# Shifting where a matmul kernel's buffers stand in SBUF, by multiples of 64 bytes

## The chip, the cores and the metric

The kernel runs on one core of a Trainium2 chip. The metric is the device time of one execution in microseconds; 1243.23 us is the median of two runs of the kernel before (1243.19 to 1243.27). One more execution was taken with the hardware profiler and is the source of every row below.

## The reference

Two transformer-like blocks run one after the other on 256 tokens of width 1024, in float32. Cut to what matters:

```
# first block
h = rmsnorm(x); proj = h @ w_in                       # 1024 x 8192
branches = conv mixer, stick-breaking attention, retention   # each 512 wide
x = x + (sum_n sigmoid(gates_n) * (branch_n @ w_branch_n)) @ w_o
x = x + memory_attention(rmsnorm(x), rmsnorm(mem), w_xq, w_xkv, w_xo)
x = x + relu(rmsnorm(x) @ w_up)**2 @ w_down           # 1024 x 4096 x 1024
x = rmsnorm(x)
# second block
h = layer_norm(a*h + ssd_mixer(h))                    # in 1024 x 6176, out 2048 x 1024
h = layer_norm(a*h + conv_ffn(h))                     # up 1024 x 5632, down 2816 x 1024
h = layer_norm(a*h + mla_attention(h))                # latents 384 and 256 wide
h = layer_norm(a*h + conv_ffn(h))
```

## The kernel before, in words

**Three matmuls for one.** Each float32 operand is held as a high part in the float32r format and a rest. A product is formed as high x high, high x rest and rest x high, accumulated in PSUM (`mm3`, with `passes = ((0, 0), (0, 1), (1, 0))`). Every one of these matmuls loads its own stationary operand of 128 columns (LDWEIGHTS) and then streams 256 or 512 moving columns of 4 bytes.

**The weights.** They come from DRAM in about 200 chunks of up to 128 x 2048 elements, through three rings that `pump`, `copy` and `sub` serve: `wr` (raw, two buffers, by DMA), `wh` (high parts, four buffers, written by ScalarE) and `wl` (rests, four buffers, written by VectorE). Method `ring` makes each buffer; each is 8192 bytes of a partition.

**Which operand streams.** In `wstat` the weights are loaded and the activations stream, 256 columns at a time: this is the up projections, gates, queries and keys. In `xstat` the activations are loaded and the weights stream, mostly 512 columns at a time: this is the down and output projections. `wmixed` does the first three chunks of an up projection with streaming weights of 256 columns.

**The activations.** `new_act` gives each layer a pair `ah`, `al` (128 x 8 x 256 elements each, high and rest). It is called seven times: for the mixers, the memory attention's queries, the MLP, the SSD mixer, the first FFN, the latent attention, the second FFN. Other stationary or moving operands have pairs of their own: `br` (the three branches), `mt` (merged) and `memT` (the memory), `gT` (the hidden layer of MLP and FFN), `yT` (SSD), `oT` (attention outputs), `cT` (latents).

**The order of the work.** A planner in the program (`Plan`, `tick`, `step`) decides, when the program is built, in which order each engine's instructions are written; it uses modelled costs and never a buffer's address. The buffers' addresses follow from the order in which the pools are opened and from `gap`, which allocates so many unused bytes.

**A word used below.** The *place* of a buffer is its byte address in a partition, modulo 512. Before, `wr`, `wh` and `wl` all stand at place 288, `ah` and `al` at 480, `br`, `gT`, `yT` and the memory attention's `oT` at 288, `mt`, `memT`, `cT` and the latent attention's `oT` at 480. The *distance* of an operand is its place minus that of `wh`, modulo 512. Within a buffer, a step from one 128-row slice to the next is a multiple of 512 bytes in every case named here, so one distance holds for a whole stage.

Of the kernel before, what the change touches and what calls it, by code (L numbers as in the profile page):

```python
# [7 lines left out]
F32R = mybir.dt.float32r  # L8
# [8 lines left out]
P = 128  # L17
D = 1024
S = 256
ALPHA = 4 ** 0.25  # L20
NG = 8
RAW, HELD = 2, 4
# [198 lines left out]
class Slots:  # L221
    def __init__(self, kern, pool, name, shape, dtype, n):
        self.kern, self.at, self.pool, self.name, self.shape, self.dtype = kern, kern.at, pool, name, shape, dtype
        self.idle = list(range(n))
        self.out, self.old, self.lent = {}, {}, {}
# [237 lines left out]
        self.sync = Lane(plan, nc.sync, "sp")  # L463


class Kern:
    def __init__(self, nc, tc, a, dbg=None):
        self.at = Plan()
        self.nc, self.tc, self.a, self.dbg = Engines(nc, self.at), tc, a, dbg
        self.plan, _ = chunk_plan()  # L470
        self.nch = len(self.plan)
        self.n_dma = self.n_prep = self.n_half = self.n_get = self.n_done = 0
        self.raw, self.held, self.subs = {}, {}, []
        self.bg = []
        self.floor = 0.0
        self.turns = {}
        self.blocked, self.table = False, None
        self.work = self.skew = 0.0
        self.sums = np.concatenate([[0.0], np.cumsum([len(ks) * max(n, P) * UNIT for _, ks, _, n, _ in self.plan])])

# [12 lines left out]
            self.n_dma += 1  # L493

    def ring(self, pool, tag, dtype, n):
        t = pool.tile([P, 2048], dtype, tag=tag, name=tag)
        rows = self.turns.setdefault(tag, [])
        self.at.reuse(t, rows[-n] if len(rows) >= n else None)
        rows.append(t)
        return t  # L500
# [316 lines left out]

    def new_act(self):

        return (self.acts.tile([P, 8, S], F32R, tag="ah", name="ah"), self.acts.tile([P, 8, S], F32R, tag="al", name="al"), [0, 0])  # L820

    def ready(self, act, k, *taus):
        if len(act) == 3:
# [132 lines left out]
    def mixers(self, act):  # L956
        nc, a = self.nc, self.a
        mp, mp_close = self.open("mix")
        br = self.pair(mp, "br", 12)
        gt = Slots(self, mp, "gt", [P, 3, S], F32, 4)  # L960
        r256 = Slots(self, mp, "r256", [P, 256], F32, 6)
# [267 lines left out]
        for m in range(8):  # L1229
            wh, wl = self.get("br")  # L1230
# [534 lines left out]
    def attention(self, h, act):  # L1765
        nc = self.nc
        cos, sin = self.cs[:, 0], self.cs[:, 1]
        pool, close = self.open("mla")
        self.gap(pool, 704)
        cT = self.pair(pool, "cT", 5)  # L1770
        krT = pool.tile([P, S], F32, tag="krT", name="krT")
        knT = pool.tile([P, 8, S], F32, tag="knT", name="knT")
# [100 lines left out]
        for tau in range(2):  # L1873
            for tag, nk, src, blocks in (("qr", 3, cq, [(0, 512)]), ("v", 2, ckv, [(0, 512), (512, D)])):
                if tau == 0:
                    chs[tag] = self.get(tag)
                wh, wl = chs[tag]
# [90 lines left out]
    def program(self):  # L1968
        nc, tc, a = self.nc, self.tc, self.a
        cs = []  # L1970

        def pool(name, bufs=1, **kw):
            cm = tc.tile_pool(name=name, bufs=bufs, **kw)
            cs.append(cm)
            return cm.__enter__()

        cp = pool("const")
        self.gb = pool("gb", 2)  # L1980
        self.dram = pool("dram", space=bass.MemoryType.DRAM)
        self.acts = pool("acts")
        cq = pool("small")
        self.tiny = pool("tiny", 4)
        self.tk = Slots(self, pool("tk"), "tk", [P, D], F32, 2)
        self.wraw, self.whi, self.wlo = pool("wraw", RAW), pool("whi", HELD), pool("wlo", HELD)
        pp = pool("ps", space=PSUM)
        self.mm = Slots(self, pp, "mm", [P, 512], F32, 4)
        self.sm = Slots(self, pp, "sm", [P, 512], F32, 4)

        x = cp.tile([P, 2, D], F32, tag="x", name="x")
        self.cst = cst = cq.tile([P, NCST], F32, tag="cst", name="cst")
        self.ones = cp.tile([P, P], F32, tag="ones", name="ones")
        nc.vector.memset(self.ones, 1.0)

        row = self.tk.get()
        o, w = ROWS["mix"]
        nc.sync.dma_start(out=row[0:1, :], in_=a["prow"][0:1, o:o + w])
        halves = [slice(512 * n, 512 * n + 512) for n in range(2)]
        for c in halves:  # L2000
            nc.sync.dma_start(out=x[:, 0, c], in_=a["x"][0:P, c])
        nc.sync.dma_start(out=cst[:, 0:P], in_=a["cst"][:, 0:P])
        self.pump(1)
        nc.sync.dma_start(out=x[:, 1, :], in_=a["x"][P:2 * P, :])
        self.pump()
        nc.sync.dma_start(out=cst[:, P:], in_=a["cst"][:, P:])
        gs = [self.mm.get() for c in halves]
        for pt, c in zip(gs, halves):
            self.mm1(pt, self.ones[0:1, :], row[0:1, c], True)
        self.tk.put(row)  # L2010
        self.pcol = cp.tile([P, NCOL], F32, tag="pcol", name="pcol")
        nc.sync.dma_start(out=self.pcol, in_=a["pcol"])
        self.ident, self.nu, self.ut = (cst[:, CST[n]:CST[n] + P] for n in ("ident", "nu", "ut"))
        self.at.one = cq.tile([1, 2], F32, tag="one", name="one")
        nc.vector.memset(self.at.one, 1.0)
        self.neg1 = cp.tile([P, P], F32, tag="neg1", name="neg1")
        nc.vector.memset(self.neg1, -1.0)
        self.mhalf = cq.tile([P, 2], F32, tag="mhalf", name="mhalf")
        nc.vector.memset(self.mhalf, -0.5)
        self.identb = cp.tile([P, P], BF16, tag="identb", name="identb")  # L2020
        nc.vector.tensor_copy(self.identb, self.ident)

        self.maskb = cp.tile([P, P], BF16, tag="maskb", name="maskb")
        nc.vector.memset(self.maskb, 0.0)
        nc.gpsimd.affine_select(out=self.maskb, in_=self.maskb, compare_op=ALU.is_ge, fill=-1e30, base=0,
                                pattern=[[-1, P]], channel_multiplier=1)

        act = self.new_act()
        self.until(self.spawn(self.rms(0, x, Halves(gs), act), first=True))

        def second():
            yield from self.rms(1, x, Halves(gs), act)
            for pt in gs:
                self.mm.put(pt)

        self.spawn(second(), first=True)
        mt, memT, mt_close = self.mixers(act)
        self.spawn(self.angles(cp))
        act, close = self.memory(x, mt, memT, mt_close)
        act = self.mlp(x, act, close)  # L2040
        act = self.ssd(x, act)
        act = self.ffn(0, x, act)
        act = self.attention(x, act)
        self.ffn(1, x, act)
        self.drain()
        assert self.n_get == self.nch
        for cm in reversed(cs):
            cm.__exit__(None, None, None)
# [21 lines left out]
```

## Time and profile before

| | |
|---|---|
| median of two runs | 1243.23 us |
| the profiled execution | 1244.83 us, span 1243.1 us |
| TensorE (PE) | 1224.7 us busy, 8468 matmuls |
| weight loads (PEld) | 1120.8 us busy, beside the matmuls |
| VectorE (DVE) | 853.9 us busy |
| ScalarE (ACT) | 717.0 us busy |
| DMA | 227.71 MB, mean 183 GB/s |

A matmul's row shows its start and its modelled duration, 0.28 us for 256 columns; it overlaps the next one's. The pace of a stretch is therefore the time from one start to the next, not the duration. Where a row gives a stretch and a count, the count also holds the two matmuls or so that were under way at the stretch's start.

### The profile page before, as it was taken

The page shows a single profiled execution, that of the slowest core. Times are in us where ns is not written, and L with a number is a line of the kernel's source. Part 1 is how long each engine was busy: PE and PEld are TensorE (multiplying, and loading weights), DVE is VectorE, ACT ScalarE, POOL GpSimd, SP SyncE. Part 2 cuts the span into 40 slices and gives each one's busy share as a digit, 9 for nine tenths or more (in the row PEclk, how much of TensorE's full clock was granted, in tenths as well). Part 3 has the DMA queues.
Part 4 walks back from the last instruction along what each step waited for, and adds up shares of the span by engine and source line. Part 5 has one row for each costly group of instructions (what it writes and reads, how often), then busy time and mean ns, then how long its engine had stood idle before and what let it go on. Part 6 is the DMA issues. An engine that isn't in the chain of part 4 may idle for free.

```text
span 1243.1 us, 20768 instructions
## 1 busy us (share of the span) xinstructions
PE 1224.7 (99%) x8468; PEld 1120.8 (90%) x8468; DVE 853.9 (69%) x1378; ACT 717.0 (58%) x1181; POOL 53.5 (4%) x85
## 2 busy tenths in 40 slices
PE   7999999999999999999999999999999999999997
PEld 5978999989989998889999898999988888999986
DVE  5666847666746665446787797877765866888853
ACT  5666546446536554335788765666644575666641
POOL 0011000000000000000111201000000000000000
PEclk9999999999999999999999999999999999999999
DMA  7643355546544546524656555555573443455560
GB/s 254 235 167 127 146 196 219 179 156 228 176 152 159 214 172 221 201 106 166 227 190 233 193 174 194 187 172 202 184 259 118 161 181 123 172 197 182 213 256 35
DMA packets 35425, 227.71 MB, mean 183 GB/s; under 512 B 4321, under 2 KB 4993, under 8 KB 11522
## 3 DMA queue, kind: packets, MB, share of 16 engines
q1 hardware_dynamic: 35330, 226.39, 50.8%
q8 instruction: 66, 1.08, 0.4%
q14 instruction: 29, 0.24, 0.1%
HBM read 225.27 MB, written 1.10 MB: 182 GB/s over the span
## 4 chain that ended last, share of the span: by engine, by line
PE 95%; DVE 3%; DMA 1%; issue 0%; ACT 0%; POOL 0%; SPq 0%; POOLq 0%; DVEq 0%; ACTq 0%
PE mm L284 85%; PE sm L284 9%; DVE wl L284 1%; DVE x L284 1%; DMA wr<-wts 0%; DVE tk L284 0%; DMA cst<-cst 0%; POOL rs L284 0%; ACT wh L284 0%; DVE ln L284 0%; DVE al L284 0%; SPq L284 0%; POOLq L2066 0%; ACT r L284 0%; ACT ah L284 0%
## 5 line engine op out<-in xcount | busy, mean ns | idle before, releaser
L284 DVE TENSOR_TENSOR wl<-wr,wh 128x1024 fp32r<-128x1024 f32 (+3 forms) x408 | 479.4, 1198 | 173.7 <-ACT wh L284 173.0
L284 ACT CAST wh<-wr 128x1024 fp32r<-128x1024 f32 (+3 forms) x408 | 403.6, 1029 | 162.4 <-PE mm L284 87.9
L284 PE MATMUL mm<-ah,wh 128*128 128x256 f32 (+1 forms) x1496 | 421.1, 281 | 0.0
L284 PE MATMUL mm<-ah,wl 128*128 128x256 f32 (+1 forms) x1496 | 417.5, 279 | 0.0
L284 PE MATMUL mm<-al,wh 128*128 128x256 f32 (+1 forms) x1496 | 417.4, 279 | 0.0
L284 PEld LDWEIGHTS mm<-ah,wh 128*128 128x128 f32 (+1 forms) x1496 | 283.0, 189 | 1.6 <-issue 1.1
L284 PEld LDWEIGHTS mm<-ah,wl 128*128 128x128 f32 (+1 forms) x1496 | 281.0, 188 | 0.1
L284 PEld LDWEIGHTS mm<-al,wh 128*128 128x128 f32 (+1 forms) x1496 | 280.5, 188 | 0.4
L284 DVE SCALAR_TENSOR_TENSOR r<-mm,pcol,r 128x255 f32<-128x255 f32 (+2 forms) x212 | 86.9, 474 | 38.6 <-ACT r L284 38.6
L284 PE MATMUL mm<-wl,ah 128*128 128x512 f32 (+3 forms) x320 | 106.3, 338 | 3.1 <-DVE wl L284 3.0
L284 PE MATMUL mm<-wh,ah 128*128 128x512 f32 (+3 forms) x320 | 108.6, 345 | 0.0
L284 PE MATMUL mm<-wh,al 128*128 128x512 f32 (+3 forms) x320 | 105.9, 337 | 0.5 <-DVE al L284 0.5
L284 PE MATMUL mm<-wh,gTh 128*128 128x512 f32 x304 | 96.3, 391 | 0.0
L284 PE MATMUL mm<-wh,gTl 128*128 128x512 f32 x304 | 95.6, 389 | 0.0
L284 PE MATMUL mm<-wl,gTh 128*128 128x512 f32 x304 | 95.6, 390 | 0.0
L284 ACT ACTIVATE r<-mm,pcol 128x256 f32<-128x256 f32 x96 | 48.9, 560 | 46.9 <-PE mm L284 46.9
L284 PEld LDWEIGHTS mm<-wl,ah 128*128 128x128 f32 x320 | 60.3, 189 | 10.2 <-DVE wl L284 4.9
L284 PEld LDWEIGHTS mm<-wh,gTl 128*128 128x128 f32 x304 | 57.1, 188 | 11.8
L284 PEld LDWEIGHTS mm<-wl,gTh 128*128 128x128 f32 x304 | 57.1, 188 | 11.8
L284 PEld LDWEIGHTS mm<-wh,gTh 128*128 128x128 f32 x304 | 56.7, 188 | 12.0 <-issue 0.6
L284 PEld LDWEIGHTS mm<-wh,al 128*128 128x128 f32 x320 | 60.3, 189 | 7.0 <-DVE al L284 1.1
L284 PEld LDWEIGHTS mm<-wh,ah 128*128 128x128 f32 x320 | 60.3, 189 | 6.6 <-issue 0.7
(296 smaller groups left out, 1581.8 us busy)
## 6 DMA issues: line engine op xcount, KB each, us to landing
wr<-wts SPq DMA_DIRECT2D x186, 1024.0 KB, 4.9
wr<-wts SPq DMA_DIRECT2D x11, 768.0 KB, 4.3
gb<-prow SPq DMA_DIRECT2D x12, 512.0 KB, 6.8
dec<-rows SPq DMA_DIRECT2D x8, 768.0 KB, 7.5
wr<-wts SPq DMA_DIRECT2D x4, 704.0 KB, 4.2
wr<-wts SPq DMA_DIRECT2D x4, 512.0 KB, 7.0
tk<-mem SPq DMA_DIRECT2D x2, 512.0 KB, 7.9
out<-x SPq DMA_DIRECT2D x4, 256.0 KB, 2.1
```

The lines of the kernel that those rows point to most:

```text
L284: r = f(*args, **kw)
```

## The change: what it does

No instruction is added, removed or moved: the program that is built holds the same instructions in the same order with the same waits on every engine. Only addresses change.

- `ring` makes each `wl` buffer 64 bytes longer (`PLACE` elements of 4 bytes), so the four stand at places 480, 32, 96 and 160. With `gap0` in front, `wr` and `wh` stand at 480; all four of each still do.
- `new_act` allocates 128 elements more and lets the layer's activations begin `PLACES[n]` bytes further on, with another value for each of its seven calls. The high part and the rest move alike.
- Gaps of 320 bytes place the branches `br` and the latents `cT` (with the latent attention's `oT`) at 288.
- The scratch for dynamic DMA descriptors is cut from 16384 to 1024 bytes, which makes the room.

Distances from `wh` (bytes, modulo 512), worked out from the allocations of the two programs:

| operand | before | after |
|---|---|---|
| `ah`, `al`: mixers, memory queries | 192 | 64, 64 |
| `ah`, `al`: MLP | 192 | 320 |
| `ah`, `al`: SSD | 192 | 192 |
| `ah`, `al`: first FFN | 192 | 448 |
| `ah`, `al`: latent attention | 192 | 0 |
| `ah`, `al`: second FFN | 192 | 128 |
| `br` | 0 | 320 |
| `cT`, latent attention's `oT` | 192 | 320 |
| `mt`, `memT` | 192 | 0 |
| `gT`, `yT`, memory attention's `oT` | 0 | 0 |
| `wl`, by ring position | 0, 0, 0, 0 | 0, 64, 128, 192 |

```
+PLACE = 16
+PLACES = (64, 64, 320, 192, 448, 0, 128)
...
+        self.n_act = 0
...
     def ring(self, pool, tag, dtype, n):
-        t = pool.tile([P, 2048], dtype, tag=tag, name=tag)
+        t = pool.tile([P, 2048 + (PLACE if tag == "wl" else 0)], dtype, tag=tag, name=tag)
...
     def new_act(self):
-        return (self.acts.tile([P, 8, S], F32R, tag="ah", name="ah"), self.acts.tile([P, 8, S], F32R, tag="al", name="al"), [0, 0])
+        at = PLACES[self.n_act] // 4
+        self.n_act += 1
+        h, l = (self.acts.tile([P, 8 * S + 128], F32R, tag=n, name=n)[:, at:at + 8 * S].rearrange("p (k s) -> p k s", s=S) for n in ("ah", "al"))
+        return (h, l, [0, 0])
...
         mp, mp_close = self.open("mix")
+        self.gap(mp, 320)
         br = self.pair(mp, "br", 12)
...
         pool, close = self.open("mla")
-        self.gap(pool, 704)
+        self.gap(pool, 320)
...
-        self.wraw, self.whi, self.wlo = pool("wraw", RAW), pool("whi", HELD), pool("wlo", HELD)
+        self.gap(pool("gap0"), 192)
+        self.wraw, self.whi = pool("wraw", RAW), pool("whi", HELD)
+        self.wlo = pool("wlo", HELD)
+        self.gap(pool("gap1"), 256)
...
-    nc = bacc.Bacc("TRN2", target_bir_lowering=False, num_devices=1)
+    nc = bacc.Bacc("TRN2", target_bir_lowering=False, num_devices=1, dynamic_dma_scratch_size=1024)
```

## Rows read from the trace of the kernel before

**Rows 1.** The page's head and the engines' busy time (share of the span).
```profile
span 1243.1 us, 20768 instructions
...
PE 1224.7 (99%) x8468; PEld 1120.8 (90%) x8468; DVE 853.9 (69%) x1378; ACT 717.0 (58%) x1181; POOL 53.5 (4%) x85
```

**Rows 2.** The page's chain that ended last: shares of the span by engine, by line.
```profile
PE 95%; DVE 3%; DMA 1%; issue 0%; ACT 0%; POOL 0%; SPq 0%; POOLq 0%; DVEq 0%; ACTq 0%
PE mm L284 85%; PE sm L284 9%; DVE wl L284 1%; DVE x L284 1%; DMA wr<-wts 0%; DVE tk L284 0%; DMA cst<-cst 0%; POOL rs L284 0%; ACT wh L284 0%; DVE ln L284 0%; DVE al L284 0%; SPq L284 0%; POOLq L2066 0%; ACT r L284 0%; ACT ah L284 0%
```

**Rows 3.** Matmul groups by form, one of three passes each (shape, xcount | busy us, ns).
```profile
L284 PE MATMUL mm<-ah,wh 128*128 128x256 f32 x1488 | 418.9, 281 | 0.0
...
L284 PE MATMUL mm<-wh,gTh 128*128 128x512 f32 x304 | 96.3, 391 | 0.0
...
L284 PE MATMUL mm<-wh,ah 128*128 128x512 f32 x144 | 59.0, 410 | 0.0
...
L284 PE MATMUL mm<-wh,ah 128*128 128x256 f32 x144 | 41.0, 285 | 0.0
...
L284 PE MATMUL mm<-brh,wh 128*128 128x256 f32 x96 | 27.3, 285 | 0.0
...
L284 PE MATMUL mm<-memTh,wh 128*128 128x256 f32 x64 | 17.8, 278 | 0.0
```

**Rows 4.** Stretches of one kind: us, busy PE (matmuls), granted clock, DMA share, GB/s.
```profile
140.00:180.00 40.00, 40.00 (x355) 1.00 0.56 198
198.00:208.00 10.00, 10.00 (x87) 1.00 0.68 264
238.00:250.00 12.00, 12.00 (x102) 1.00 0.58 199
282.00:295.00 13.00, 13.00 (x117) 1.00 0.48 181
384.00:390.00 6.00, 6.00 (x54) 1.00 0.61 199
400.00:470.00 70.00, 70.00 (x596) 1.00 0.55 196
505.00:545.00 40.00, 40.00 (x179) 1.00 0.51 188
576.00:584.00 8.00, 8.00 (x70) 1.00 0.37 126
663.00:668.00 5.00, 5.00 (x47) 1.00 0.38 125
797.00:893.00 96.00, 96.00 (x818) 1.00 0.52 179
1076.00:1166.00 90.00, 90.00 (x797) 1.00 0.53 183
```

**Rows 5.** PE's timeline in the first FFN: first and last of 50 rows (start, us).
```profile
819.82 0.28 PE L284 MATMUL mm<-ah,wh 128*128 128x256 f32 x1
...
825.59 0.28 PE L284 MATMUL mm<-al,wh 128*128 128x256 f32 x1
```

**Rows 6.** The same in the second FFN: first and last of 50 rows.
```profile
1099.79 0.28 PE L284 MATMUL mm<-ah,wh 128*128 128x256 f32 x1
...
1105.34 0.28 PE L284 MATMUL mm<-al,wh 128*128 128x256 f32 x1
```

**Rows 7.** PE's timeline, weights streaming against `ah` (SSD): first and last of 21 matmuls.
```profile
640.70 0.40 PE L284 MATMUL mm<-wh,ah 128*128 128x512 f32 x1
...
645.37 0.40 PE L284 MATMUL mm<-wh,al 128*128 128x512 f32 x1
```

**Rows 8.** The same against `mt` (output projection): first and last of 41 matmuls.
```profile
255.76 0.39 PE L284 MATMUL mm<-wh,mtl 128*128 128x512 f32 x1
...
264.91 0.39 PE L284 MATMUL mm<-wh,mth 128*128 128x512 f32 x1
```

**Rows 9.** The page's DMA queues.
```profile
q1 hardware_dynamic: 35330, 226.39, 50.8%
```

## The prediction, made before the changed kernel ran

> **What bounds the kernel now.** I read the page first: TensorE is busy for 1224.7 us of 1243.1 [rows 1], and the chain that ended last lies on PE for 95%, on VectorE for 3% [rows 2]. So nearly every nanosecond between two matmul starts is a nanosecond of the kernel. No row of DVE, ACT or DMA can pay for this change; only the pace of the matmuls can.
>
> Next come the groups of matmuls by form, for the counts [rows 3]. A row is one of three passes, so streaming activations of 256 columns number 3 x 1488 = 4464; streaming weights of 256 columns 432, branches 288, memory 192; of 512 columns, weights against `gT` 912 and against `ah` 432.
>
> Then the stretches of one kind [rows 4], where the reader is to see that equal work does not go at an equal pace. With two matmuls taken off each count for those under way at the start:
> - at distance 192, activations of 256 columns take 40 us / 353 = 113.3 ns in the gates (140 to 180 us) and 90 / 795 = 113.2 in the second FFN, but 70 / 594 = 117.8 in the MLP and 96 / 816 = 117.6 in the first FFN. The timelines say the same over 49 starts each: 5.55 us / 49 = 113.3 [rows 6] and 5.77 / 49 = 117.8 [rows 5];
> - the gates themselves also go at 10 / 85 = 117.6 from 198 us on, and the SSD stage at 117.6 (576 to 584 us) and at some 112 (663 to 668 us);
> - at distance 0, the branches take 12 / 100 = 120.0, while the memory at distance 192 takes 13 / 115 = 113.0;
> - streaming weights of 256 columns, with `ah` loaded, take about 6 / 51 = 117.6 (three taken off).
>
> [...] The two FFNs run the same code at the same places, so 113.3 and 117.8 are two lasting paces of one arrangement; 120.0 came with another distance. That is what ties the place to the pace.
>
> For 512 columns: 40 / 177 = 226.0 ns against `gT` (distance 0), 9.15 / 40 = 228.8 against `mt` [rows 8] and 4.67 / 20 = 233.5 against `ah` in the SSD stage [rows 7], these two at 192.
>
> My reading, which the rows suggest and do not prove: while one operand streams, the next one is loaded, both out of SBUF, and they meet in the same part of it for a time set by the distance and by the moment at which the load began.
>
> [...] The rows show 120.0 and 113.0 ns for the same shape at the same clock [rows 4]. [...]
>
> **The change, part by part.** Instructions, their order and their waits stay, so each term is a count times a change of pace.
> 1. *Streaming activations, 4464.* Surely at the long pace now: queries and keys 192, MLP 13 x 48 = 624, first FFN 19 x 48 = 912, together 1728 (the first 192 by the likeness of their stage, not by a row). At the short pace: second FFN 912, memory queries 192. In between: convolution 288, gates 576, SSD 768, together 1632, of which I take half at either. So 2544 go at 117.8 and 1920 at 113.3, mean 115.9. The new distances 64, 128, 320 and 448, and 192 with rests that stand 0, 64, 128 or 192 further on, occur in no long stretch of the trace. Bounds: 113.3 and 120.0, the ends of what is seen for this shape. I take 113.3, the lower of the two paces seen away from distance 0, because a long pace that lasts 96 us needs every pair of operands to stand alike, and now one pair in three changes its distance with each chunk. That gives 2544 x 4.5 ns = -11.4 us. Where a rest comes to distance 0 from the operand that streams, I charge 120.0: in one chunk of four, one matmul of three, in the stages at 64, 128 and 192 (1056 + 192 + 912 + 768 = 2928), that is 244 x 6.7 = +1.6 us. Sum -9.8; bounds 2544 x -4.5 = -11.4 and 4464 x 4.1 = +18.3.
> 2. *Branches, 288*, from distance 0 to 320: from 120.0 to between 113.3 and 117.8, middle 115.5, -1.3 us.
> 3. *Memory keys, 192*, from 192 to 0: two thirds at 120.0, of the rest a quarter, 144 x 6.7 = +1.0 us. This part is a plain loss.
> 4. *Streaming weights, 432*: 117.6 to the same middle, -0.9 us; bounds 113.3 and 120.0, -1.9 and +1.0.
> 5. *512 columns against `ah`, 432*: now between 228.8 and 233.5, middle 231; I take 228.8, -1.0 us; bounds 226.0 and 233.5, -2.2 and +1.1.
> 6. *512 columns against `gT`, 912*: two thirds stay at distance 0. The streaming rests, 304, move to 0, 64, 128, 192 behind; a quarter stays, 228 may go to 228.8, +0.6 us; bounds 0 and 228 x 7.5 = +1.7.
> 7. *`mt`, `memT`, latents* go to 0 or 320 with some 300 matmuls: gains and losses of at most 7 ns each, taken as zero, bounds -1 and +1 us.
> 8. *The scratch.* [...] Zero; if a descriptor needed it, the kernel would wait for DMA where PE waits for nothing now. DVE and ACT read and write at new places too; they lie beside PE.
>
> Sum: -9.8 - 1.3 + 1.0 - 0.9 - 1.0 + 0.6 = -11.4 us. The profiled execution took 1244.8 us (its span 1243.1 and 1.7 around it), which is 1.6 above the median; 1244.8 - 11.4 - 1.6 gives **1232 us**.
>
> **The rivals.**
> - *Nothing moves on the whole.* Which pace a stage falls into hangs on the moment at which it starts, as the two FFNs show at equal places; then the change only deals the paces again. For it: the gates change pace within the stage. Against it: distance 0 has its own pace. Time: 1243, within 4 us. [...]
> - *The stagger makes the slow meeting the rule.* Place: streaming activations while a rest is loaded, a third of 4464. If with four different distances each ring position finds its own bad moment, these 1488 go at 120.0 and the other 2976 stay at 117.8, mean 118.5 instead of 115.9: +11.6 us, with +1.0 for the memory and +1.7 for `gT`: 1257 us. It decides once the mean of the 4464 is above about 116.3 ns, where the other terms' 1.6 us are eaten. For it: long paces are common now, and only the one arrangement in which all rests stand alike is seen to hold 113.3 for 90 us.
> - *Some distances meet nowhere.* [...] Against it: no long stretch of the trace goes under 113.
>
> **How the numbers follow.** Chances: the forecast 0.60 (1223 to 1240, from the bounds of terms 1 to 6 with part or all of the 117.8 gone), nothing moves 0.20 (1239 to 1247), slower 0.10 (1247 to 1262), meets nowhere 0.10 (1195 to 1222). The range 1218 to 1250 leaves out most of the last and half of the slower case, about 0.15. Two per cent, about what a measurement of this kernel can tell from no change, is 25 us: under 1218 only in the last case, 0.10; over 1268 only if terms 1 and 6 all go to their bad ends, 0.02; within, 0.88.
>
> **What would show it.** Right: the stretches that correspond to 400 to 470 and 797 to 893 us show 113 to 114 ns a start, the branches under 118, the memory keys near 120, and PE stays at 95% of the chain. Term 1 is wrong if the first FFN still goes at 117.8 or the second leaves 113.3. The no-change rival shows as stages that swap paces with the same sum; the slower one as starts that are long where a rest is loaded and short elsewhere; the last as stretches below 113. Wrong altogether would be a time that changes with PE's paces unchanged: then DVE, ACT or DMA paid, which I put at nothing.

## The result, and the profile after

The changed kernel takes 1256.5 us (median of two runs, 1256.22 to 1256.78) against 1243.23: a ratio of 1.0123, 95% interval 1.0082 to 1.0164. It is slower, clear of the measurement, though by less than two per cent. The forecast was 1232 us and the range ended at 1250.

The page's head and busy row after, beside [rows 1], and the first row of its chain, beside [rows 2]:

```profile
span 1254.5 us, 20769 instructions
...
PE 1237.9 (99%) x8468; PEld 1128.4 (90%) x8468; DVE 853.6 (68%) x1378; ACT 717.6 (57%) x1181; POOL 53.6 (4%) x85
...
PE 95%; DVE 2%; DMA 1%; issue 0%; ACT 0%; POOL 0%; SPq 0%; POOLq 0%; DVEq 0%; ACTq 0%
```

The span grew by 11.4 us and PE's busy time by 13.2, with the same 8468 matmuls; DVE and ACT are as busy as before to 0.6 us. So the time went where it was expected to be decided, into the pace of the matmuls. The one instruction more in the head is a semaphore event on GpSimd, so that "no instruction is added", as the change was described, holds for PE, DVE and ACT but not to the last one. The stretches that answer to [rows 4], in the windows view (us, busy PE with its matmuls, clock, DMA share, GB/s), are the gates, the branches, the memory keys, the MLP, a hidden layer (512 columns), the first and the second FFN:

```profile
141.00:181.00 40.00, 40.00 (x342) 1.00 0.55 197
240.00:252.00 12.00, 12.00 (x103) 1.00 0.57 183
285.00:297.00 12.00, 12.00 (x103) 1.00 0.48 181
430.00:474.00 44.00, 44.00 (x375) 1.00 0.50 182
509.00:549.00 40.00, 40.00 (x176) 1.00 0.55 197
803.00:893.00 90.00, 90.00 (x780) 1.00 0.51 182
1090.00:1176.00 86.00, 86.00 (x729) 1.00 0.54 186
```

With two matmuls taken off each count: gates 40 / 340 = 117.6 ns (113.3 before), branches 118.8 (120.0), memory 118.8 (113.0), MLP 118.0 (117.8), hidden layer 229.9 (226.0), first FFN 115.7 (117.6), second FFN 118.3 (113.2). The granted clock is 1.00 in all of them, before and after, so it is not the clock.

For the sums I took, from the trace's starts, the mean time from one matmul to the next over each whole stage, leaving out gaps of over 139 ns at 256 columns and of over 277 ns at 512 (about 7340 intervals in each kernel):

| stage (intervals) | before | after | step of 64 alone | distances alone | step of 128 alone | last kernel |
|---|---|---|---|---|---|---|
| mixers, 256 columns (1023) | 115.0 | 117.9 | 115.9 | 117.1 | 113.7 | 113.6 |
| branches (284) | 119.8 | 118.1 | 118.7 | 114.6 | 119.4 | 113.5 |
| memory keys (190) | 113.5 | 118.7 | 115.7 | 119.9 | 113.6 | 113.6 |
| memory queries (188) | 113.7 | 116.9 | 116.4 | 117.9 | 114.1 | 114.1 |
| MLP (622) | 117.7 | 117.6 | 116.3 | 117.8 | 113.5 | 113.5 |
| SSD, 256 columns (752) | 116.0 | 116.5 | 116.3 | 114.7 | 114.4 | 114.6 |
| first FFN (910) | 117.7 | 115.7 | 115.7 | 113.4 | 113.4 | 113.4 |
| second FFN (910) | 113.4 | 118.2 | 115.7 | 120.0 | 113.5 | 113.4 |
| hidden layers, 512 columns (900) | 226.9 | 230.0 | 229.9 | 226.9 | 228.5 | 226.8 |
| all stages together, us | 1062.7 | 1075.1 | 1069.1 | 1068.2 | 1055.8 | 1050.7 |

After less before, the second FFN gives 910 x 4.8 ns = +4.4 us, the mixers +3.0, the hidden layers +2.8, memory keys and queries +1.6, SSD +0.4; the first FFN gives back 1.8, the branches 0.5, the MLP 0.1. The other stages hold +2.6 of the +12.4.

### The profile page after: what moved, and what is told of

Same layout as the page of the kernel before. It is cut to its first block, busy times and chain, and to the rows that moved or that the text cites. A ratio compares the mean times of both kernels' runs of the same rounds, so it can differ in the third digit from the quotient of the medians.

```text
span 1254.5 us, 20769 instructions
## 1 busy us (share of the span) xinstructions
PE 1237.9 (99%) x8468; PEld 1128.4 (90%) x8468; DVE 853.6 (68%) x1378; ACT 717.6 (57%) x1181; POOL 53.6 (4%) x85
## 2 busy tenths in 40 slices
DMA packets 35425, 227.71 MB, mean 182 GB/s; under 512 B 4321, under 2 KB 4993, under 8 KB 11522
## 4 chain that ended last, share of the span: by engine, by line
PE 95%; DVE 2%; DMA 1%; issue 0%; ACT 0%; POOL 0%; SPq 0%; POOLq 0%; DVEq 0%; ACTq 0%
PE mm L284 86%; PE sm L284 9%; DMA wr<-wts 1%; DVE wl L284 1%; DVE x L284 0%; DVE al L284 0%; ACT wh L284 0%; DVE tk L284 0%; POOL rs L284 0%; DVE ln L284 0%; SPq L284 0%; POOLq L2078 0%; ACT r L284 0%; DVEq L2078 0%; DVE mth L284 0%
## 5 line engine op out<-in xcount | busy, mean ns | idle before, releaser
L284 PEld LDWEIGHTS mm<-wh,gTl 128*128 128x128 f32 x304 | 57.0, 187 | 13.2
```

Source lines behind the costliest of these rows:

```text
L284: r = f(*args, **kw)
```

## The experiments

Two theories at first. Theory S: the stagger of the rests breaks the short pace. Theory D: the new distances are long in themselves. All kernels keep the changed kernel's small scratch, and each was timed against the kernel before on the same chip.

**The step of 64 alone.** Everything at its place of before, but the rests' step kept:

```
-PLACES = (64, 64, 320, 192, 448, 0, 128)
+PLACES = (0, 0, 0, 0, 0, 0, 0)
-        self.gap(mp, 320)
-        self.gap(pool, 320)
+        self.gap(pool, 704)
-        self.gap(pool("gap0"), 192)
```

> Every buffer at its place of before, but the four buffers of the weights' rests 64 bytes further on each (distances 0, 64, 128, 192 from the high parts). Theory S (the stagger breaks the short pace): about the changed kernel's time, 1250 to 1258 us, and the second FFN goes at 117 to 118.5 ns a start instead of 113.3. Theory D (the new distances of activations, branches and latents are slow in themselves): 1241 to 1246 us, the second FFN stays at 113.3.

Measured: ratio 1.0076 (1.0058 to 1.0094), 1250.18 us. The second FFN went from 113.4 to 115.7, short of S's 117 to 118.5, and the first fell from 117.7 to the same 115.7. Its windows show why. These are four consecutive chunks of the second FFN, 48 matmuls each:

```profile
1085.07:1090.52 5.45, 5.45 (x50) 1.00 0.53 192
1090.52:1096.17 5.65, 5.65 (x51) 1.00 0.54 190
1096.17:1101.63 5.46, 5.46 (x51) 1.00 0.54 192
1101.63:1107.29 5.66, 5.66 (x50) 1.00 0.55 185
```

The chunks stand at ring positions 0, 3, 2, 1, and 5.45, 5.65, 5.46 and 5.66 us over 48 are 113.5, 117.7, 113.8 and 117.9 ns. The pattern repeats with every turn of the ring, in both FFNs. The changed kernel shows it to the hundredth in its first FFN, at distance 448:

```profile
821.35:826.80 5.45, 5.45 (x50) 1.00 0.58 198
826.80:832.45 5.65, 5.65 (x51) 1.00 0.51 183
832.45:837.91 5.46, 5.46 (x51) 1.00 0.56 198
837.91:843.57 5.66, 5.66 (x50) 1.00 0.48 184
```

So at ring positions 1 and 3 each of the three matmuls of a product is longer, 4 ns on the mean, and not one in three: by the starts, the three passes take 116.0 to 119.4 ns there. At positions 0 and 2 almost nothing is lost.

Two readings fit these chunks. Either the rest stands badly to its high part, 64 or 192 bytes off, or it stands badly to the operand that streams: with that operand at distance 192, the rests at positions 1 and 3 come to 128 and 0 from it. The branches of the same run tell the two apart, because they stand at distance 0, where positions 1 and 3 bring the rest to an odd multiple of 64 from the stream. By the starts, they go at 119.8, 117.9, 119.1 and 117.8 ns at positions 0 to 3: shorter, not longer, where the rest stands 64 or 192 from its high part. The memory keys of the changed kernel, also at distance 0, do the same (119.6, 118.3, 119.1, 117.9). That speaks for the rest's own distance to the stream; the changed second FFN, at 128, is less clean (118.6, 116.9, 118.5, 118.8).

**The distances alone.**

```
-PLACE = 16
+PLACE = 0
-        self.gap(pool("gap1"), 256)
```

> The changed kernel with the four buffers of the rests at one place again, so that each stage has one distance: mixers and memory queries 64, MLP 320, SSD 192, first FFN 448, latents' input 0, second FFN 128, branches 320. Theory S: at or below the time of before, 1230 to 1244 us, with steady paces of 113.3 or 117.8 in long stretches. Theory D: 1250 to 1258 us, the second FFN at 117 to 118.5 ns as in the changed kernel.

Measured: ratio 1.0068 (1.0050 to 1.0087), 1248.83 us: outside both ranges, nearer to D's, and the second FFN was longer than D expected; the step had its own cost as well, as the run before showed. MLP (320), first FFN (448), second FFN (128):

```profile
410.00:460.00 50.00, 50.00 (x427) 1.00 0.56 202
800.00:890.00 90.00, 90.00 (x797) 1.00 0.53 186
1082.00:1170.00 88.00, 88.00 (x736) 1.00 0.52 181
```

That is 117.6, 113.2 and 119.9 ns. Against the kernel before on the same chip (1240.97 us) the step alone costs 9.2 us and the distances alone 7.9; both together cost 13.3, less than the sum. In the second FFN the step even helps: 120.0 with the distances alone, 118.2 in the changed kernel.

**Other distances.** The same with `PLACES = (320, 256, 64, 448, 256, 128, 384)`.

> As the run before it, one distance in each stage, but others: mixers 320, memory queries 256, MLP 64, SSD 448, first FFN 256, latents' input 128, second FFN 384. Theory S: the pace of a stage without stagger is one of the lasting ones, 113.3, 117.8 or 120.0 ns, whatever the distance, and 120.0 only at distance 0; 1230 to 1250 us. Theory D: pace goes by distance, and distances other than 192 go at 117 or more; 1250 to 1262 us.

Measured: ratio 1.0120 (1.0097 to 1.0143), 1256.15 us, the time that D expected. MLP (64), first FFN (256), second FFN (384):

```profile
410.00:460.00 50.00, 50.00 (x427) 1.00 0.54 191
805.00:895.00 90.00, 90.00 (x752) 1.00 0.50 177
1090.00:1174.00 84.00, 84.00 (x710) 1.00 0.52 184
```

That is 117.6, 120.0 and 118.6. With one distance in a stage, 0, 128, 256 and 384 go at 118.6 to 120.0, 64 and 320 mostly at 117 to 118, 192 and 448 at 113.3 or 117.8 in the long stretches (D's "distances other than 192 go at 117 or more" fails for 448: the SSD stage there has a mean of 114.7). The branches at 320 were an exception, 114.6 in this run and the one before. Distances 256 bytes apart mostly go alike, the widest gap being 120.0 at 128 and 118.6 at 384, so the runs sort them roughly by their remainder modulo 256.

**A step of 128 alone.** As the step of 64 alone, with `PLACE = 32` and no `gap1`.

> Every buffer at its place of before, but the rests' buffers step by 128 bytes instead of 64 (distances 0, 128, 256, 384 from the high parts). Theory P (what counts is whether high part and rest stand an even or an odd multiple of 64 bytes apart): no ring position goes at 117.6 to 118; all four go at 113 to 114.5 in the 256-column stages, also in MLP and first FFN, which were at 117.8; against the hidden layer (512 columns) the staggered positions cost up to 4 ns; 1232 to 1240 us. Theory A (any difference between high part and rest breaks the short pace): 1248 to 1255 us, as with the step of 64.

Measured: ratio 0.9961 (0.9943 to 0.9979), 1238.07 us, ten runs within 1237.36 to 1239.24. The time and the long stages are as theory P had them; only the branches, at distance 0, stayed at 119.4. The MLP, then four consecutive chunks of the first FFN, then the second FFN:

```profile
410.00:460.00 50.00, 50.00 (x443) 1.00 0.55 203
816.37:821.81 5.44, 5.44 (x50) 1.00 0.53 196
821.81:827.25 5.44, 5.44 (x50) 1.00 0.54 193
827.25:832.69 5.44, 5.44 (x50) 1.00 0.54 194
832.69:838.13 5.44, 5.44 (x50) 1.00 0.53 196
1076.00:1160.00 84.00, 84.00 (x744) 1.00 0.54 193
```

All are at 113.2 to 113.4, the MLP for the first time. With the stream at 192, a step of 128 keeps every rest at an odd multiple of 64 from the stream too, so this run fits both readings above. The hidden layers lose 1.6 ns.

**A step of 256**, `PLACE = 64`.

> As the run before it with a step of 256 bytes (distances 0, 256, 0, 256). Theory P: as with 128, 1230 to 1240 us, and less lost against the hidden layer. Theory A: two ring positions of four disturbed, 1244 to 1250 us.

Measured: 0.9994 (0.9970 to 1.0018), 1241.88 us. Neither theory: the stages go at the two old paces again, MLP, first FFN, second FFN:

```profile
410.00:460.00 50.00, 50.00 (x426) 1.00 0.52 186
800.00:890.00 90.00, 90.00 (x796) 1.00 0.52 188
1082.00:1166.00 84.00, 84.00 (x715) 1.00 0.53 188
```

117.9, 113.4, 117.8: in the kernel before it was long, long, short [rows 4]. A step of 256 is no step. It also suggests that the pace of a stage is dealt anew in each execution: ten runs of this kernel gather near 1239.5 and 1243.6, with one each at 1245.3 and 1248.1, and 25 runs of the kernel before on that chip near 1239.5, 1243.4 and 1247.5. One FFN at the other pace is 912 x 4.5 ns = 4.1 us. That the runs differ by such a stage is inferred, since only one execution of each was profiled. The profiled ones fit: 1243.61 us here with the MLP and one FFN long, 1240.04 in the next run with the MLP alone. These kernels keep the small scratch and are as fast as the kernel before (0.9994 and 0.9999), so the scratch costs nothing that shows.

**Distance 448 throughout**, branches at 320, no step.

```
-PLACE = 16
-PLACES = (64, 64, 320, 192, 448, 0, 128)
+PLACE = 0
+PLACES = (256, 256, 256, 256, 256, 256, 256)
-        self.gap(pool, 320)
+        self.gap(pool, 704)
-        self.gap(pool("gap0"), 192)
-        self.gap(pool("gap1"), 256)
```

> No stagger; all seven activations at distance 448, branches at 320, all else at the distances of before. Theory P (448 and 192 are the two good distances, alike modulo 256, and 448 has no lasting long pace): MLP, both FFNs and memory queries at 113.3 to 114, 1230 to 1236 us. Theory T (the short pace of the first FFN at 448 was an accident of the moment at which it started, as with 192 before): at least one of MLP, first and second FFN at 117.8, 1236 to 1245 us.

Measured: 0.9999 (0.9975 to 1.0023), 1240.35 us: theory T. Both FFNs went at 113.4, the MLP at 117.6:

```profile
410.00:460.00 50.00, 50.00 (x427) 1.00 0.52 189
800.00:890.00 90.00, 90.00 (x797) 1.00 0.53 188
1082.00:1160.00 78.00, 78.00 (x690) 1.00 0.54 193
```

**Odd multiples of 32.** As the one before, with `PLACES = (32, 352, 416, 480, 480, 352, 32)` and no gap for the branches.

> No stagger; the activations at odd multiples of 32 bytes from the weights: mixers 224, memory queries 32, MLP 96, SSD 160, first FFN 160, latents' input 32, second FFN 224; all else as before. Theory G (only whole steps of 64 bytes count, and what stands across two of them meets in either): no pace under 113, most stages at 117 to 121, 1245 to 1262 us. Theory F (a finer grid, or 113.3 itself contains a loss by standing 32 bytes off a multiple of 64): at least one stage under 112.5 ns, 1225 to 1243 us.

Measured: 1.0122 (1.0088 to 1.0155), 1259.15 us: theory G. MLP (96) and first FFN (160) at 119.9 and 118.6; no stage of streaming activations at an odd multiple of 32 is under 116 (the memory keys, left at 192, stay at 113.5):

```profile
412.00:462.00 50.00, 50.00 (x419) 1.00 0.54 197
805.00:895.00 90.00, 90.00 (x761) 1.00 0.49 173
```

**The change with a step of 128.** `PLACE = 32` in the changed kernel, without `gap1`.

> The changed kernel with one number changed: the rests step by 128 bytes instead of 64. Theory P (a lasting long pace needs all rests alike, and a step of 64 spoils every other ring position): the stages at odd multiples of 64 (mixers and memory queries 64, MLP 320, SSD 192, first FFN 448, branches 320) go at 113.3 to 115.5; only the second FFN (128), the memory keys (0) and the latents' input stay at 118 to 120; 1240 to 1245 us. Theory D (64 and 320 are long in themselves): mixers, memory queries and MLP stay at 117 to 118, 1247 to 1252 us.

Measured: 1.0046 (1.0030 to 1.0062), 1247.32 us: on D's edge by time, split by stage. MLP (320), first FFN (448), second FFN (128):

```profile
410.00:460.00 50.00, 50.00 (x444) 1.00 0.57 202
800.00:890.00 90.00, 90.00 (x796) 1.00 0.53 188
1082.00:1170.00 88.00, 88.00 (x742) 1.00 0.52 187
```

The MLP falls from 117.6 without a step to 113.1, so 320 is not long in itself; but the mixers (117.0 over their whole stage) and the memory queries (118.4), both at 64, stay long. By the remainder modulo 256, 64 and 320 are one class; why they part here is open.

**Towards the better kernel.** First the step of 128 with the branches moved to 192 (`self.gap(mp, 192)`).

> The run with the step of 128, and the branches moved from distance 0 to 192. Theory P: the 288 matmuls of the branches go from 119.4 to 113.3 to 114.5 ns, 1.4 to 1.8 us less than with the step alone, 1236 to 1237.5 us, and the runs lie within 2 us of each other, since no stage is left that can stay at 117.8 through its whole length. Theory A: the branches stay above 117, 1238 us.

Measured: 0.9952 (0.9935 to 0.9969), 1235.87 us, just under P's range, six runs within 1.0 us. Half of the branches' matmuls stand in one stretch:

```profile
231.60:247.60 16.00, 16.00 (x143) 1.00 0.60 219
```

Over their whole stage they go at 113.5. Then the step only where activations stream:

```
-PLACE = 32
+PLACE = 128
+STEP = 32
+STREAMED = ("qk", "conv", "gate", "br", "xk", "xq", "up", "ssd", "dt", "fu", "kn", "qn")
...
-            self.held[c] = (self.ring(self.whi, "wh", F32R, HELD), self.ring(self.wlo, "wl", F32R, HELD))
+            o = STEP * (c % 4) if self.plan[c][0] in STREAMED else 0
+            self.held[c] = (self.ring(self.whi, "wh", F32R, HELD), self.ring(self.wlo, "wl", F32R, HELD)[:, o:o + 2048])
```

> As the run with the step of 128 and the branches at 192, but the rests step only in chunks against which activations stream; where the weights stream (512 columns) all rests stand at one place again, inside wider buffers. Theory P: the 256-column stages stay at 113.3 to 114.5 ns, the hidden layers go back from 228.5 to 226.8, about 1.5 ns for each of 1500 to 1900 matmuls, so 2 to 3 us less: 1232.5 to 1234.5 us. Theory A: the long pace of a 256-column stage can begin again in the stretches without steps and last into the next stage; a stage at 117.8, 1236 to 1241 us.

Measured: 0.9939 (0.9917 to 0.9961), 1234.37 us, in P's range, the fastest of all and below both kernels. It is 1.5 us less than the run before it, on another chip, where 2 to 3 were expected. MLP, hidden layer, first and second FFN:

```profile
410.00:460.00 50.00, 50.00 (x444) 1.00 0.52 190
500.00:540.00 40.00, 40.00 (x179) 1.00 0.52 187
800.00:880.00 80.00, 80.00 (x708) 1.00 0.55 194
1076.00:1150.00 74.00, 74.00 (x656) 1.00 0.55 190
```

113.1, 226.0, 113.3 and 113.1: each, to 0.1 ns, at the shortest pace that a long stretch of its shape showed before, 113.2 and 226.0.

## Why the prediction was wrong

**The bound was right.** Only PE's pace moved: PE's idle time in the span even fell, from 18.4 to 16.6 us, and DMA moved the same 227.71 MB. The two lasting paces at one arrangement were read rightly from [rows 5] and [rows 6], and so was the mean of the 4464: 115.9 by the prediction, 115.7 by the starts. Two small readings were off: the stretch at "some 112" (663 to 668 us) goes at 113.4 by its starts, and the 233.5 of [rows 7] is one stretch of a shape whose mean is 230.0.

**Term 1 failed**, by its sentence that the new distances and the stagger would leave 113.3. It gave -9.8 us; its stages measured +6.5 (mixers +3.0, queries +0.6, MLP -0.1, SSD +0.4, first FFN -1.8, second FFN +4.4), within its bounds of -11.4 and +18.3. Three things were in it:
- That a long pace needs every rest to stand alike was borne out at distance 192: a step of 128 leaves no long pace in MLP and FFNs, and ten runs of that kernel lie within 1.9 us, where 25 of the kernel before spread over 10.3. At distance 64 it was not: mixers and memory queries stay long with that step. And it was taken for any step, where 64 is the wrong one.
- The charge for a bad pair was put on one matmul of three (6.7 ns); the chunk shows some 4 ns on each of the three, about 13 together, and at two ring positions of four, not one: a rest at 128 from the stream costs as a rest at 0 does (117.9 and 117.7 ns in the chunks of the step of 64).
- The unknown distances got the value 113.3 from the two rows at 192. Of the four new ones, 64 and 128 go at 117 to 120, and 320 went at 117.6 in the MLP. The one other distance then in the rows, 0 at 120.0, was the warning: the mean of the bounds, 116.6, would have made the term about +3.

**Term 6** was +0.6 and measured +2.8. Its upper bound, +1.7, was broken for the same reason: by the starts, the hidden layers go at 227.0 ns at ring position 0 and at 230.5 to 231.2 at the three others, and there all three matmuls of a product are longer, also the two that don't read the rest.

**The small terms.** Branches: -1.3 forecast, -0.5 measured. Memory keys: +1.0 and +1.0, the one term that rested on a row at its own distance. Streaming weights of 256 columns: -0.9 and +0.4. 512 columns against `ah`: -1.0 and +0.7. Term 7: 0 and +1.7, with the outputs of the SSD and the memory attention, which no term had. Term 8, the scratch: 0 and nothing seen: with 1024 bytes of it the step of 256 and distance 448 ran at 0.9994 and 0.9999 of the kernel before; whether the kernel's DMAs use it, no run shows. Together +12.6 against -11.4.

**The rivals.** The slower rival named the time, 1257, and the place, and its stages are long at ring positions of their own; but it expected 120.0 on the third that meets and 117.8 on the rest, where, in the first FFN, two positions are spoiled whole and two are short. That its time fits is partly luck: it gave the 4464 matmuls +11.6 us, they measured +6.5, and terms that it left out filled the gap. "Nothing moves" had a part, by inference: paces seem to be dealt anew where all rests stand alike, worth about 4 us a stage. But places do change the pace: with PE's instructions equal, the second FFN goes at 113.4 in the kernel before and at 120.0 with the distances alone. "Meets nowhere" found no support: no run shows the pace that its 1195 to 1222 us would need. No stage of 256 columns went under 113; the shortest long stretches, at 113.1, were the MLP with the change and a step of 128, and the MLP and the second FFN of the last kernel.

**The range** was too short above: it left out half of the slower case at a chance of 0.10, though term 1's own upper bound reached further.

What stays argued is the cause below the paces: that a streaming read and the load of the next operand meet in SBUF. The runs tie it to distances between operands, but no run took the loads away. The other engines and DMA can be set aside as what is met: in the run with other distances, the first FFN holds its 120.0 ns in the 67 intervals with no VectorE, ScalarE or GpSimd instruction under way, and in the 245 with no DMA packet under way (each from 250 ns before the interval on).

## What to carry to other kernels

When PE is the bound and each matmul loads its own operand, measure the time from start to start per stage: here, at 256 columns and a granted clock of 1.00, the second FFN went at 113.4 ns at distance 192 and at 120.0 at 128. Treat the place of every operand modulo 256 bytes, or better 512, as a parameter (with no step, 128 and 384 went at 120.0 and 118.6; with the step of 128, the mixers at 64 went at 117.0 and the MLP at 320 at 113.1), for streams of 256 and of 512 columns apart, and try it on the chip one stage at a time, since a value without a row of its own is worth the middle of its bounds, not the better end. Before comparing runs a few microseconds apart, see whether a stage can hold either of two paces; where it holds one only, as with the step of 128, runs lie closer together (ten within 1.9 us, against 25 within 10.3) and small differences can be read.

## What the runs showed of the hardware that was not expected

- One stage can hold 113.3 or 117.8 ns a matmul for 80 us and more at the same addresses; with rests that step by 128 bytes the MLP and the FFNs went at 113.1 to 113.5 wherever they stood at 192 or 448.
- Streams of 256 columns with no step are shortest at distances 192 and 448 (113.3) and longest at 0, 128 and 256 (120.0). Streams of 512 columns with no step are shortest at 0 (226.8 in the hidden layers, up to 228.4 in small stages) and take 229 to 233.5 elsewhere.
- A rest at one of the long distances lengthens all three matmuls of a product: with the step of 64, ring positions 1 and 3 of the first FFN go at 118.0 and 117.6 as a whole, 0 and 2 at 113.6 and 113.8.
- Odd multiples of 32 bytes never helped: 116.7 to 120.0 ns for streaming activations.
